# Group norm's mean moved from the recurrence's output to the value projection

## The chip, the cores and the metric

The kernel runs on one NeuronCore of a Trainium2 chip. TensorE (PE, with its weight loads PEld), VectorE (DVE), ScalarE (ACT) and GpSimd (POOL) each work through a queue of their own in a fixed order. SyncE (SP) issues nearly all DMAs, also in order. The metric is device time in microseconds (us) of one execution.

## The reference, cut to what matters

The model is a trunk of two layers on 1024 tokens of width 1024: an RWKV-7 time mixer, then differential attention, each followed by a gated per-layer embedding. The change lies in the first layer. Each of its 16 heads (64 wide) keeps a 64x64 state that a delta rule updates from token to token. The state's output `y` goes through a group norm of each head:

```
proj = einsum('bsgd,dgc->bsgc', xm, w_in)          # r, k, v, gate
def step(state, inp):
    sa    = einsum('bhij,bhj->bhi', state, kk_t)
    state = state * w_t - sa[..., None] * b_t + v_t[..., None] * k_t
    y_t   = einsum('bhij,bhj->bhi', state, r_t)
...
mean = jnp.mean(y, axis=-1, keepdims=True)          # over the 64 of a head
var  = jnp.mean(jnp.square(y - mean), axis=-1, keepdims=True)
y    = (y - mean) * rsqrt(var + GN_EPS) * ln_w + ln_b
bonus = sum(rh * kh * r_k, axis=-1, keepdims=True) * vh
y    = (y + bonus) * silu(gate) @ w_out
```

The index `i` of `state[i, j]` comes only from `v`, and every step is linear in it. So the mean of `y` over a head is what the same recurrence would give from the mean of `v` over that head. The bonus uses `v` as it is.

## The kernel before, in words

**Stages.** The span falls into these: norm and low-rank projections, then the projections of k and r, then **the v stage** (331 to 457 us), then the gate projection (to 572 us), then **the scan** over 16 chunks of 64 tokens with group norm and output projection woven in (to about 940 us), then the second half of the first layer, attention, and the tail.

**The v stage.** It runs over 4 column blocks `q` of 256 and 8 token blocks `i` of 128, 32 blocks in all. Each has 24 matmuls into a PSUM tile of tag `mm` (4 buffers), one ACT copy of 128x256 into an SBUF tile `vst` (L664) and one DMA from SP to the scratch tensor `v_d` (L665). `vst` takes a buffer of the tag `xmt`, of which there are 3; `make_xm`, which prepares the inputs of the next projection (L221), takes its buffers from the same 3. Woven between these blocks and the gate projection by `tick` are the triangular inverses that the scan needs: `inv_pb` (PE and DVE), `inv_diag` with a long chain of small DVE operations `tm`, `tb` (L558, L560) and two transposes (L570, L575), and `inv_merge` (PE products `pg` and `po`, L593, fed by ACT copies `prhs` and `pairs`). They come in four quarters.

**The scan.** For chunk c, `chain_x`, `chain_u` and `chain_s` are the recurrence; `stage1` prepares chunk c+1, with `mh` giving `pm` on PE (L185) and the masked `m` on DVE (L188). `vload` reads v of a chunk (L837). After every second chunk `d1_pieces` normalises 128 tokens: `norm` (a DVE reduction, a small scale and a subtraction, L953 to L955, then a square on ACT, L957), `norm2` (from L963), `turn` (PE transposes `ytr`, L981) and the output projection `op`. It also loads v (L944) for the bonus. ACT writes `y` from PSUM at L923. `d1_pieces` runs 8 times.

**Order.** The program is written in the order of these pieces, and a planner with its own estimates of cost settles the order on each engine. That order is fixed before the run, and an engine waits at an instruction until its inputs and its buffer are there.

Of the kernel before, what the change touches and what calls it, by code (L numbers as in the profile page):

```python
# [11 lines left out]
F32 = mybir.dt.float32  # L12
# [3 lines left out]
AF = mybir.ActivationFunctionType  # L16
ALU = mybir.AluOpType
AX = mybir.AxisListType
# [3 lines left out]
P = 128  # L22
D = 1024
SEQ = 1024
KT = D // P
NT = SEQ // P
L = 64
# [10 lines left out]
def trunk(ctx: ExitStack, tc: tile.TileContext, A, out):  # L38
    nc = tc.nc
    V, S, G, T = nc.vector, nc.scalar, nc.gpsimd, nc.tensor  # L40

    cp = ctx.enter_context(tc.tile_pool(name="const", bufs=1, reuse_waits="tile"))
    dp = ctx.enter_context(tc.tile_pool(name="scratch", bufs=1, space=DRAM))
# [8 lines left out]
    kb_d = dp.tile([KT, P, NCH, 2, L], F32, name="kb_d")  # L52
    kkr_d = dp.tile([KT, P, NCH, 2, L], F32, name="kkr_d")
    v_d = dp.tile([SEQ, D], F32, name="v_d")
    sg_d = dp.tile([KT, P, SEQ], F32, name="sg_d")

    def rsqrt(y, a, t):
# [9 lines left out]
    def mean_eps(ms, ss, n, eps):  # L67
        V.tensor_scalar(out=ms, in0=ss, scalar1=1.0 / n, scalar2=eps, op0=ALU.mult, op1=ALU.add)
# [5 lines left out]
    def mm3(ps, ah, al, bh, bl, start, stop):  # L74
        T.matmul(ps, lhsT=ah, rhs=bh, start=start, stop=False)  # L75
        T.matmul(ps, lhsT=ah, rhs=bl, start=False, stop=False)  # L76
        T.matmul(ps, lhsT=al, rhs=bh, start=False, stop=stop)  # L77
# [19 lines left out]
    ssn = cp.tile([P, NT, 16], F32, name="ssn")  # L97
# [95 lines left out]
    with NB("ab") as ab, NP("psab") as pp:  # L193
# [23 lines left out]
        def wpair(nm):  # L217
            return (ab.tile([P, D], F32R, tag="wh", name=nm + "h", bufs=3),
                    ab.tile([P, D], F32R, tag="wl", name=nm + "l", bufs=3))
# [14 lines left out]
        def make_half(g, hf):  # L234
            return [make_xm(g, kt, hf) for kt in range(KT)]

        def wload(nm, src):
            r = wraw(nm + "r")
            nc.sync.dma_start(out=r, in_=src)
            h, lo = wpair(nm)  # L240
            split(h, lo, r)
            return h, lo
# [21 lines left out]
        with NB("pl") as pl:  # L264
# [56 lines left out]
            for nm, cf in (("c", cA), ("p", cB)):  # L321
                t = wraw("lw" + nm).rearrange("p (k c) -> p k c", c=P)
                for g in range(2):
                    gs = slice(g * L, g * L + L)
                    V.tensor_tensor(out=t[:, :, gs], in0=wa[:, :, gs],
                                    in1=cf[:, 4 + g].unsqueeze(2).to_broadcast([P, KT, L]), op=ALU.mult)
                h, lo = wpair("lws" + nm)
# [308 lines left out]
        def tick(n):  # L636
            due[0] += n
            while due[0] >= 1.0:
                due[0] -= 1.0
                next(bg, None)  # L640
# [10 lines left out]
        for q in range(4):  # L651
            wv = [wload(f"wv{q}{k2}", A["wv"][q, k2].rearrange("p k c -> p (k c)")) for k2 in range(2)]
            for i in range(NT):
                x_ = xm[i // 4]
                ts_ = slice((i % 4) * P, (i % 4 + 1) * P)
                ps = pp.tile([P, 512], F32, tag="mm", name=f"v{q}{i}", bufs=4)[:, 0:256]
                for kt in range(KT):
                    if kt == 4 and (q or i > 3):
                        tick(TV)
                    cs = slice((kt % 4) * 256, (kt % 4) * 256 + 256)  # L660
                    mm3(ps, x_[kt][0][:, ts_], x_[kt][1][:, ts_], wv[kt // 4][0][:, cs], wv[kt // 4][1][:, cs],
                        kt == 0, kt == KT - 1)
                st = ab.tile([P, 512], F32, tag="xmt", name=f"vst{q}{i}", bufs=3)[:, 0:256]
                S.copy(st, ps)  # L664
                nc.sync.dma_start(out=v_d[i * P:(i + 1) * P, q * 256:(q + 1) * 256], in_=st)  # L665
                if q or i > 2:
                    tick(TV)
                if q == 3 and i % 4 == 3:
                    new[i // 4] = make_half(3, i // 4)
# [146 lines left out]
    with NB("d") as d, NP("psco") as pp:  # L816
# [17 lines left out]
        def vload(c):  # L834
            vu = co.tile([P, 2, 4, 2, L], F32, tag="vu", name=f"vu{c}", bufs=2)
            for st in range(2):
                nc.sync.dma_start(out=vu[64 - 64 * st:128 - 64 * st, st].rearrange("p j h l -> p (j h l)"),  # L837
                                  in_=v_d[c * L:(c + 1) * L, st * 512:st * 512 + 512])
            vus[c] = vu

        half_ = lambda x: slice(64 * x, 64 * x + 64)
# [1 line left out]
        def chain_x(c):  # L843
# [3 lines left out]
            if c + 1 < NCH:  # L847
                vload(c + 1)
# [87 lines left out]
        def d1_pieces(i):  # L936

            w = D1[i]
            rows = slice(i * P, (i + 1) * P)
            y = w["y"]  # L940

            def load():
                w["v"] = dt_("vn", f"vn{i}")
                nc.sync.dma_start(out=w["v"], in_=v_d[rows, :])  # L944
                w["sg"] = kview(dt_("sg", f"sg{i}"))
                nc.sync.dma_start(out=w["sg"], in_=sg_d[:, :, rows].rearrange("j p t -> p j t"))
                w["x"] = dt_("xr", f"xr{i}")
                nc.sync.dma_start(out=w["x"], in_=A["x"][rows, :])

            def norm():  # L950
                y3 = y.rearrange("p (h l) -> p h l", l=L)
                st = d.tile([P, 4, 16], F32, tag="gst", name=f"gst{i}", bufs=2)
                V.tensor_reduce(out=st[:, 0], in_=y3, axis=AX.X, op=ALU.add)  # L953
                V.tensor_scalar(out=st[:, 0], in0=st[:, 0], scalar1=-1.0 / L, scalar2=None, op0=ALU.mult)
                V.tensor_tensor(out=y3, in0=y3, in1=st[:, 0].unsqueeze(2).to_broadcast([P, 16, L]), op=ALU.add)  # L955
                sq = dt_("sq", f"ysq{i}")
                S.activation(sq, y, AF.Square)  # L957
                w["st"], w["sq"] = st, sq

            def norm2():  # L960
                st, sq, vn = w["st"], w["sq"], w["v"]
                y3 = y.rearrange("p (h l) -> p h l", l=L)
                V.tensor_reduce(out=st[:, 1], in_=sq.rearrange("p (h l) -> p h l", l=L), axis=AX.X, op=ALU.add)  # L963
                mean_eps(st[:, 1], st[:, 1], L, 64e-5)
                rsqrt(st[:, 2], st[:, 1], st[:, 3])
                V.tensor_tensor(out=y3, in0=y3, in1=st[:, 2].unsqueeze(2).to_broadcast([P, 16, L]), op=ALU.mult)
                G.tensor_tensor(out=y, in0=y, in1=lnw, op=ALU.mult)
                v3 = vn.rearrange("p (h l) -> p h l", l=L)
                G.tensor_tensor(out=v3, in0=v3, in1=bon[:, i].unsqueeze(2).to_broadcast([P, 16, L]), op=ALU.mult)
                V.tensor_tensor(out=y, in0=y, in1=vn, op=ALU.add)  # L970
                w["gh"] = kview(dt_("gh", f"gh{i}", 2, F32R))
                w["gl"] = kview(dt_("gl", f"gl{i}", 2, F32R))
                w["ps"] = [None, None]

            def turn(hf):
                yg, gh, gl = w["sg"], w["gh"], w["gl"]
                ps = pp.tile([P, 4, P], F32, tag="t", name=f"ytr{i}{hf}", bufs=2)
                hs = slice(hf * 4, hf * 4 + 4)
                for q in range(4):
                    kt = hf * 4 + q  # L980
                    T.transpose(ps[:, q], y[:, kt * P:(kt + 1) * P], ident)  # L981
                for q in range(4):
                    kt = hf * 4 + q
                    V.scalar_tensor_tensor(out=yg[:, kt], in0=ps[:, q], scalar=vec["ln_b"][:, kt:kt + 1],
                                           in1=yg[:, kt], op0=ALU.add, op1=ALU.mult)
                split(gh[:, hs], gl[:, hs], yg[:, hs], V)

            def mms(hf, k0):
                gh, gl = w["gh"], w["gl"]
                cs = slice(hf * 512, hf * 512 + 512)  # L990
                if k0 == 0:
                    w["ps"][hf] = pp.tile([P, 512], F32, tag="mm", name=f"op{i}{hf}", bufs=2)
                for kt in range(k0, k0 + 2):
                    mm3(w["ps"][hf], gh[:, kt], gl[:, kt], wo[kt][0][:, cs], wo[kt][1][:, cs],
                        kt == 0, kt == KT - 1)
                if k0 + 2 == KT:
                    V.tensor_tensor(out=w["x"][:, cs], in0=w["ps"][hf], in1=w["x"][:, cs], op=ALU.add)
                    if hf == 1:
                        nc.sync.dma_start(out=h1_d[rows, :], in_=w["x"])
                        sq = dt_("sq", f"h1sq{i}")  # L1000
                        S.activation(sq, w["x"], AF.Square, accum_out=ss1[:, i:i + 1])

            def mk(hf, k0):
                return lambda: mms(hf, k0)

            m0, m1 = [[(mk(hf, k0), 1280) for k0 in range(0, KT, 2)] for hf in range(2)]
            return ([(load, 100), (norm, 1000)], [(norm2, 1000)],
                    [(lambda: turn(0), 600), (lambda: turn(1), 600)] + m0, m1)

# [625 lines left out]
```

## Time and profile before

| | |
|---|---|
| median of 3 runs | 1829.12 us (1828.71 to 1832.35) |
| profiled execution, its time | 1828.3 us |
| its span in the profile | 1826.5 us |
| mean granted TensorE clock | 0.963 |
| PE busy | 1684.7 us (92%) |
| DVE busy | 1350.9 us (74%) |
| ACT busy | 760.4 us (42%) |
| POOL busy | 634.5 us (35%) |

The span runs from the first to the last instruction; what lies around it is 1.8 us here. Busy shares are means over stages with different limits. Full granted clock is 1.00 (2.4 GHz), and 0.50 is the lower of the two levels (1.2 GHz).

### The profile page before, as it was taken

The page shows a single profiled execution, that of the slowest core. Times are in us where ns is not written, and L with a number is a line of the kernel's source. Part 1 is how long each engine was busy: PE and PEld are TensorE (multiplying, and loading weights), DVE is VectorE, ACT ScalarE, POOL GpSimd, SP SyncE. Part 2 cuts the span into 40 slices and gives each one's busy share as a digit, 9 for nine tenths or more (in the row PEclk, how much of TensorE's full clock was granted, in tenths as well). Part 3 has the DMA queues.
Part 4 walks back from the last instruction along what each step waited for, and adds up shares of the span by engine and source line. Part 5 has one row for each costly group of instructions (what it writes and reads, how often), then busy time and mean ns, then how long its engine had stood idle before and what let it go on. Part 6 is the DMA issues. An engine that isn't in the chain of part 4 may idle for free.

```text
span 1826.5 us, 30473 instructions
## 1 busy us (share of the span) xinstructions
PE 1684.7 (92%) x11320; PEld 1397.6 (77%) x11320; DVE 1350.9 (74%) x3083; ACT 760.4 (42%) x1594; POOL 634.5 (35%) x705
## 2 busy tenths in 40 slices
PE   6899999898897988898899999899999999999998
PEld 5677778887676877777678878788888888777786
DVE  7878954698994687666766747887877878856665
ACT  6566543346344332223333434444444444544332
POOL 4436644224324355455310333323323323311200
PEclk9999999998998989999999999999999999999999
DMA  7125444434225534444243411101101101431121
GB/s 267 41 61 166 129 106 109 125 102 119 73 67 186 186 127 127 122 129 131 97 172 128 132 51 39 54 7 56 56 7 56 53 10 56 154 99 34 58 93 69
DMA packets 164401, 175.97 MB, mean 96 GB/s; under 512 B 74845, under 2 KB 127837, under 8 KB 164254
## 3 DMA queue, kind: packets, MB, share of 16 engines
q1 hardware_dynamic: 161950, 169.84, 30.2%
q10 hardware_dynamic: 2304, 4.20, 0.6%
q8 instruction: 89, 1.46, 0.4%
q14 instruction: 58, 0.48, 0.1%
HBM read 124.19 MB, written 49.81 MB: 95 GB/s over the span
## 4 chain that ended last, share of the span: by engine, by line
PE 51%; DVE 10%; ACT 2%; issue 1%; DMA 0%; POOL 0%; ACTq 0%; DVEq 0%
PE qkv L75 6%; PE qkv L76 6%; PE qkv L77 6%; PE av L1359 3%; PE sc L1319 2%; PE sc L1320 2%; PE fg L75 2%; PE fg L76 2%; PE fg L77 2%; PE op L75 2%; PE op L77 2%; PE op L76 2%; PE do L75 1%; PE pg L76 1%; PE pg L77 1%; PE do L76 1%
## 5 line engine op out<-in xcount | busy, mean ns | idle before, releaser
L1329 ACT ACTIVATE e<-sc,mx 128x256 f32<-128x256 f32 (+7 forms) x128 | 94.0, 738 | 111.0 <-DVE mx L1326 60.0
L1273 POOL TENSOR_TENSOR rp<-rp,rq 128x128 f32<-128x128 f32 x64 | 34.8, 543 | 237.6 <-DVE rq L1268 189.7
L1359 PE MATMUL av<-vh,aT 128*128 128x128 f32 x576 | 81.1, 280 | 6.3 <-DVE aT L1355 6.3
L1359 PEld LDWEIGHTS av<-vh,aT 128*128 128x128 f32 x576 | 75.6, 195 | 12.8 <-DVE aT L1355 8.9
L1325 DVE TENSOR_REDUCE mxs<-sc 128x1 f32<-128x128 f32 (+6 forms) x112 | 74.2, 682 | 0.5
L1319 PE MATMUL sc<-k,q 128*128 128x512 f32 (+2 forms) x192 | 71.5, 379 | 2.2 <-ACT e L1329 2.2
L229 DVE SCALAR_TENSOR_TENSOR xmt<-hT,cB,xmt 128x512 f32<-128x512 f32 x64 | 63.5, 1012 | 6.6 <-ACT xmt L228 6.3
L1320 PE MATMUL sc<-k,q 128*128 128x512 f32 (+2 forms) x192 | 64.8, 348 | 0.0
L1361 ACT ACTIVATE o<-av,r 128x128 f32<-128x128 f32 x64 | 23.5, 367 | 88.4 <-PE av L1359 88.4
L875 POOL TENSOR_TENSOR spl<-state,plast 64x256 f32<-64x256 f32 x60 | 41.4, 690 | 49.6 <-DVE state L910 42.7
L1341 DVE SCALAR_TENSOR_TENSOR e<-e,r,e 128x128 f32<-128x128 f32 (+3 forms) x64 | 56.5, 883 | 1.2
L560 DVE TENSOR_TENSOR tb<-tb,tm 128x31 f32<-128x31 f32 (+15 forms) x124 | 53.9, 435 | 3.6
L558 DVE TENSOR_TENSOR tm<-tb,nb 128x31 f32<-128x31 f32 (+15 forms) x124 | 53.9, 434 | 3.6
L188 DVE TENSOR_TENSOR m<-pm,mmask 128x512 f32<-128x512 f32 x64 | 41.1, 682 | 20.0 <-PE pm L185 19.7
L1301 POOL CAST q<-q 64x128 fp32r<-64x128 f32 x128 | 38.5, 302 | 49.4 <-PE sc L1320 45.6
L1267 DVE TENSOR_TENSOR rp<-qkv,rc 128x256 f32<-128x256 f32 x64 | 27.1, 423 | 38.3 <-PE qkv L77 30.1
L1292 POOL CAST k<-k 64x256 fp32r<-64x256 f32 x64 | 26.1, 408 | 83.7 <-ACT k L1290 82.5
L185 PE MATMUL pm<-kkr,kb 64*128 64x128 f32 x512 | 50.8, 307 | 3.1 <-ACT kbn L176 2.2
L1355 DVE COPY aT<-at 128x512 f32<-128x512 f32 (+2 forms) x96 | 52.0, 550 | 1.1 <-PE at L1353 0.4
L185 PEld LDWEIGHTS pm<-kkr,kb 64*128 64x128 f32 x512 | 40.4, 203 | 12.9 <-issue 6.0
L1353 PE MATMUL at<-ident,e 128*128 128x128 f32 x288 | 47.4, 277 | 2.8 <-DVE e L1341 2.3
L923 ACT COPY y<-xy 64x512 f32<-64x512 f32 x32 | 18.6, 580 | 71.4 <-PE xy L916 71.0
(1180 smaller groups left out, 6001.5 us busy)
## 6 DMA issues: line engine op xcount, KB each, us to landing
pp_d<-ppo SPq DMA_DIRECT2D x32, 256.0 KB, 2.3
kb_d<-kb SPq DMA_DIRECT2D x16, 512.0 KB, 2.6
kkr<-kkr_d SPq DMA_DIRECT2D x32, 256.0 KB, 3.2
kb<-kb_d SPq DMA_DIRECT2D x32, 256.0 KB, 3.3
x<-in_x SPq DMA_DIRECT2D x8, 512.0 KB, 5.5
kkr_d<-ep SPq DMA_DIRECT2D x16, 256.0 KB, 2.6
kkr_d<-rt SPq DMA_DIRECT2D x16, 256.0 KB, 2.6
bb<-kb_d SPq DMA_DIRECT2D x32, 128.0 KB, 2.6
```

The source lines that it names most:

```text
L75: T.matmul(ps, lhsT=ah, rhs=bh, start=start, stop=False)
L76: T.matmul(ps, lhsT=ah, rhs=bl, start=False, stop=False)
L77: T.matmul(ps, lhsT=al, rhs=bh, start=False, stop=stop)
L185: ms.append(T.matmul(pm[h][:, p_], lhsT=kb[hs, p_], rhs=kkr[hs, p_], start=True, stop=True))
L229: V.scalar_tensor_tensor(out=t, in0=hT[:, kt, half(hf)], scalar=cB[:, g, kt:kt + 1], in1=t, op0=ALU.mult, op1=ALU.add)
L558: V.tensor_tensor(out=tv, in0=tb[:, j:j + 1, 0:w].to_broadcast([P, n, w]), in1=nb[:, j + 1:32, j:j + 1].to_broadcast([P, n, w]), op=ALU.mult)
L1319: T.matmul(ps[:, b0:b1], lhsT=q1[:, m, ts_], rhs=k1[:, m, b0:b1], start=True, stop=False)
L1320: T.matmul(ps[:, b0:b1], lhsT=q0[i % 2][:, m], rhs=k2[:, b0:b1], start=False, stop=True)
L1325: V.tensor_reduce(out=seed, in_=ps[:, 0:n - P], axis=AX.X, op=ALU.min)
L1329: S.activation(e[:, 0:n], ps[:, 0:n], AF.Exp, scale=-1.0, bias=mx, accum_out=l_[:, m:m + 1])
L1341: V.scalar_tensor_tensor(out=es[0][:, 0:n], in0=es[1][:, 0:n], scalar=r[:, 1:2], in1=es[0][:, 0:n], op0=ALU.mult, op1=ALU.add)
L1359: T.matmul(po, lhsT=aT[kb // 4][:, kb % 4], rhs=c["vh"][:, kb], start=(kb == 0), stop=(kb == i))
```

## The change

In the v stage ACT now evacuates each block in four pieces of 64 columns, one for each head, and sums each piece as it goes. POOL scales the four sums by -1/64 and adds them to the piece, which gives centred v beside plain v. Both go to HBM, v to `v_d` and centred v to a new scratch tensor `vc_d`. The recurrence reads `vc_d`; the bonus still reads `v_d`. In `norm` the three DVE operations fall away, and ACT squares `y` as it is.

The sums stand in `ssn`, a tile whose earlier contents have been used up by then.

```diff
+    vc_d = dp.tile([SEQ, D], F32, name="vc_d")
...
-                st = ab.tile([P, 512], F32, tag="xmt", name=f"vst{q}{i}", bufs=3)[:, 0:256]
-                S.copy(st, ps)
-                nc.sync.dma_start(out=v_d[i * P:(i + 1) * P, q * 256:(q + 1) * 256], in_=st)
+                vt = ab.tile([P, 2, 4, L], F32, tag="xmt", name=f"vst{q}{i}", bufs=3)
+                sm = ssn[:, i, 4 * q:4 * q + 4]
+                for h in range(4):
+                    S.activation(vt[:, 0, h], ps[:, h * L:(h + 1) * L], AF.Copy, accum_out=sm[:, h:h + 1])
+                G.tensor_scalar(out=sm, in0=sm, scalar1=-1.0 / L, scalar2=None, op0=ALU.mult)
+                G.tensor_tensor(out=vt[:, 1], in0=vt[:, 0], in1=sm.unsqueeze(2).to_broadcast([P, 4, L]), op=ALU.add)
+                for x, dst in enumerate((v_d, vc_d)):
+                    nc.sync.dma_start(out=dst[i * P:(i + 1) * P, q * 256:(q + 1) * 256],
+                                      in_=vt[:, x].rearrange("p h l -> p (h l)"))
...
             for st in range(2):
                 nc.sync.dma_start(out=vu[64 - 64 * st:128 - 64 * st, st].rearrange("p j h l -> p (j h l)"),
-                                  in_=v_d[c * L:(c + 1) * L, st * 512:st * 512 + 512])
+                                  in_=vc_d[c * L:(c + 1) * L, st * 512:st * 512 + 512])
...
             def norm():
-                y3 = y.rearrange("p (h l) -> p h l", l=L)
                 st = d.tile([P, 4, 16], F32, tag="gst", name=f"gst{i}", bufs=2)
-                V.tensor_reduce(out=st[:, 0], in_=y3, axis=AX.X, op=ALU.add)
-                V.tensor_scalar(out=st[:, 0], in0=st[:, 0], scalar1=-1.0 / L, scalar2=None, op0=ALU.mult)
-                V.tensor_tensor(out=y3, in0=y3, in1=st[:, 0].unsqueeze(2).to_broadcast([P, 16, L]), op=ALU.add)
                 sq = dt_("sq", f"ysq{i}")
                 S.activation(sq, y, AF.Square)
```

## Rows read from the trace of the kernel before

**Rows 1.** Busy time by stage: us, then PE, PEld, DVE, ACT, POOL, PEclk, DMA, GB/s

```profile
331.00:457.00 126.00, 116.32 (x1339) 110.08 (x1340) 100.92 (x180) 59.30 (x105) 35.15 (x23) 0.91 0.45 120
457.00:572.00 115.00, 104.45 (x714) 81.22 (x713) 95.24 (x175) 49.87 (x78) 31.37 (x22) 0.94 0.29 91
628.00:945.00 317.00, 275.70 (x3078) 230.59 (x3077) 229.13 (x453) 94.69 (x144) 153.96 (x150) 0.94 0.43 134
```

**Rows 2.** Waits of PE in the scan, 572 to 945 us: total, times, longest

```profile
PE ytr L981 <- DVE m L188: 16.8, 6, 4.1
...
PE prt L162 <- DVE m L188: 3.0, 4, 0.9
```

**Rows 3.** Timeline around one group norm: start, us, engine, line [idle before <-releaser]

```profile
705.55 1.22 DVE L953 TENSOR_REDUCE gst<-y 128x16 f32<-128x1024 f32 x1
...
706.52 0.72 POOL L157 TENSOR_TENSOR pr<-kkr,kb 128x256 f32<-128x256 f32 x1
706.80 0.48 DVE L954 TENSOR_SCALAR gst<-gst 128x16 f32<-128x16 f32 x1
707.31 1.23 DVE L955 TENSOR_TENSOR y<-y,gst 128x1024 f32<-128x1024 f32 x1
...
709.72 1.22 DVE L963 TENSOR_REDUCE gst<-ysq 128x16 f32<-128x1024 f32 x1 [1.18 <-ACT ysq L957]
710.97 1.29 DVE L188 TENSOR_TENSOR m<-pm,mmask 128x512 f32<-128x512 f32 x2
...
711.72 0.82 PE L981 MATMUL ytr<-ident,y 128*128 128x128 f32 x4 [4.04 <-DVE m L188]
```

**Rows 4.** The same columns as rows 1, after a long and a short wait

```profile
712.00:716.00 4.00, 4.00 (x44) 3.51 (x43) 2.78 (x13) 1.79 (x3) 0.73 (x1) 0.57 0.00 0
...
816.00:820.00 4.00, 3.73 (x71) 3.03 (x72) 1.41 (x3) 1.75 (x5) 3.27 (x4) 1.00 1.01 280
```

**Rows 5.** ACT by line and shape: busy us, mean ns | idle before

```profile
L1269 ACT COPY vh<-qkv 128x128 f32<-128x128 f32 x64 | 16.8, 263 | 56.0 <-DVE rq L1268 50.1 <-DVE ost L63 3.0 <-DVE ost L65 2.7
L1364 ACT ACTIVATION_READ_ACCUMULATOR os<-o 128x1 f32 x64 | 12.2, 191 | 0.0
L664 ACT COPY vst<-v 128x256 f32<-128x256 f32 x32 | 11.6, 372 | 44.6 <-PE v L77 28.4 <-issue 13.8 <-ACT pairs L567 0.9
```

**Rows 6.** POOL's nearest operations: by source line (ns min/median/max), and by line

```profile
L158 POOL TENSOR_TENSOR pr<-pr,vecs x32: 602/614/1686, 556.6 to 890.5; 128x256 f32<-128x256 f32 x32
...
L204 POOL TENSOR_SCALAR hka<-vecs 128x8 f32<-128x8 f32 x1 | 0.2, 234 | 0.0
```

**Rows 7.** Timeline of DVE and POOL in the v stage

```profile
408.10 0.42 DVE L560 TENSOR_TENSOR tb<-tb,tm 128x255 f32<-128x255 f32 x1
408.31 2.48 POOL L72 TENSOR_TENSOR wv31l<-wv31r,wv31h 128x1024 fp32r<-128x1024 f32 x1 [15.82 <-PE v L77]
408.56 2.51 DVE L558 TENSOR_TENSOR tm<-tb,nb 128x256 f32<-128x256 f32 x1
```

**Rows 8.** Timeline of PE at its waits in the v stage

```profile
331.43 0.58 PE L75 MATMUL v<-wv00h,xm_1h 128*128 128x256 f32 x1 [4.87 <-ACT vst L664]
...
389.40 2.15 PE L593 MATMUL pg<-prhs,pairs 64*64 64x32 f32 x64 [3.12 <-ACT prhs L574]
...
430.24 2.05 PE L593 MATMUL pg<-prhs,pairs 64*64 64x32 f32 x64 [1.28 <-ACT prhs L574]
```

**Rows 9.** Timeline of ACT: first and last of twenty evacuations, and the last ones

```profile
356.10 0.37 ACT L664 COPY vst<-v 128x256 f32<-128x256 f32 x1 [5.24 <-issue]
...
420.36 0.37 ACT L664 COPY vst<-v 128x256 f32<-128x256 f32 x1 [3.27 <-PE v L77]
...
454.31 0.93 ACT L664 COPY vst<-v 128x256 f32<-128x256 f32 x3
458.94 0.73 ACT L228 ACTIVATE xmt<-hT,cA 128x512 f32<-128x512 f32 x1 [3.70 <-DMA v_d<-vst]
```

**Rows 10.** Where the inverse's last transpose stands, by source line

```profile
L575 DVE STREAM_TRANSPOSE ti<-tb x4: 1867/1968/2005, 386.7 to 548.9; 128x1024 f32<-128x1024 f32 x4
```

## The prediction

> **What bounds the kernel now.** I read the busy time by stage first, because the change takes work from one stage and puts it into another. In the scan PE is busy 275.70 of 317 us, in the v stage 116.32 of 126, in the gate projection 104.45 of 115 [rows 1]. PE sets the pace in all three, and what matters is why it sometimes stands still. The list of PE's waits in the scan names one cause above the others: the transposes `ytr` wait 16.8 us in 6 places for DVE's masking `m` [rows 2]. The timeline shows what DVE does in such a place. PE stands still from 707.68, 4.04 us before 711.72. DVE first works through the three operations of the mean (705.55 to 708.54), waits 1.18 us for ACT's square, reduces it, and only then does `m` [rows 3]. So the mean stands on the path here, though DVE is busy only 229.13 of 317 us in this stage [rows 1].
>
> The v stage is bound by two things in turn. PE waits 3.12 and 1.28 us at two `pg` products for `prhs`, which ACT copies from DVE's inverse [rows 8]; there DVE sets the pace. From 457 to 572 DVE is busy 95.24 of 115 us [rows 1], and the inverse's last transpose starts at 548.9 [rows 10]: whatever delays DVE's inverse delays the scan. ACT and POOL, busy 59.30 and 35.15 of 126 us [rows 1], have room on average.
>
> **What the scan loses.** Eight groups lose 1.22, 0.48 and 1.23 us on DVE [rows 3], some 23 us in all, and the square may start as soon as `y` is there. PE's gap cannot shrink to nothing: `m` itself follows `pm`. The waits of the other chunks, where no norm stands between, are 3.0 us in 4 places, the longest 0.9 [rows 2]; I take 0.87 for what stays. The gain is 16.8 - 6 x 0.87 = 11.6 us. The clock comes on top: after a long gap it is 0.57 for 4 us, which costs 0.43 x 4 = 1.7 us, and after a short one it is 1.00 [rows 4]. Four of the six gaps are followed by such a dip, 6.8 us together; I take 5, since a dip that other waits cause would stay. The scan's gain is 16.6 us. From below it is bounded by nothing (DVE could put `norm2` in the same place), from above by the 23 us of DVE work and the 6.8 us of clock, 30 us.
>
> **What the v stage gets.** ACT's copy of 0.372 us becomes four sums of 128x64. No such row exists. Between 128x128 (0.263) and 128x256 (0.372) the step is 0.109 for 128 columns, so 64 columns should take 0.21, and at most 0.263. Each ends with a read of the accumulator, 0.191 [rows 5]. Four are 1.60 us, at most 1.82: 1.23 to 1.45 us more for a block, 39 to 46 us more in the stage. Behind them on ACT's queue are the copies for the inverse and `make_xm`.
>
> POOL gets a scale of 128x4 (nearest row 0.234) and an addition of 128x256 with a broadcast (0.614) [rows 6], 0.85 us a block, 27 us in all. Mostly it idles there, so its own time is hidden. SP gets 32 more issues, and 4.2 MB more are written (32 x 128 KB) while the DMA engines are busy 0.45 of the time [rows 1]; I count that at nothing, and it is hidden as long as inputs are loaded a block ahead. The buffer of `xmt` is held longer: by the additional 1.23 on ACT, 0.85 on POOL and one more issue, some 2.4 us.
>
> Three of these reach the path.
>
> First, PE waits at 331.43 until ACT has emptied the first block [rows 8]. Emptying takes 1.23 us longer: +1.2 (0 to 1.5).
>
> Second, DVE's inverse. While POOL runs a 2.48 us subtraction, a DVE operation that takes 0.42 next to it takes 2.51 [rows 7], so DVE loses 2.09, or 84% of POOL's time. A short one shows the same: DVE's 0.48 us scale ends with POOL's 0.72 us product [rows 3]. Of the 32 blocks, 20 are emptied between 356.10 and 420.36 [rows 9], 19 of them while DVE runs `tm` and `tb`, and the last 3 fall into its next quarter: 22. Taking 84% of 0.614, 0.5 us each, and nothing for the scale, which is so short that it mostly fits while DVE finishes its own operation, this is 11 us. It goes through to the end, because PE already waits at both `pg` and DVE has little slack after 457. If DVE's time were lost where DVE waits anyway, it is 0; if POOL's whole 0.85 counts, 19.
>
> The Trainium skill has a stricter rule here (SBUF — State Buffer, section Who interferes with whom): a DVE instruction with two SBUF inputs contends with a GpSimd instruction that reads SBUF, and whichever comes first holds the shared pair of ports for its whole length. By it, both POOL operations of a block cost DVE their whole time, 22 x 0.85 = 18.7 instead of 11. The long operation in rows 7 lies between: 84%.
>
> Third, the end of the stage. ACT empties three blocks from 454.31, and its next preparation waits 3.70 us at 458.94 for the DMA that frees a buffer [rows 9]. With buffers held 2.4 us longer, that comes about 2.5 us later, and the first gate matmuls with it: +2.5 (0 to 8).
>
> Sum: 1.2 + 11 + 2.5 = 14.7 us. The profiled execution took 1828.3 us, so 1828.3 - 16.6 + 14.7 = 1826.4 us. The median of the runs shown is 0.8 us above it; on that scale I expect 1827.0 us, 2.1 less than before.
>
> **Rivals.**
>
> The queue on ACT (slower). Between the evacuations at 420.36 and 454.31 [rows 9] ACT works mostly on copies for the inverse and on `make_xm`. If the planner puts four or more of the longer evacuations among them, each adds 1.23 us to a chain for which PE and DVE wait, 5 to 10 us, and the four blocks waiting at the start of the stage add up to 3.7 more. That is 9 to 14 on top of my sum: 1836 to 1841 us. For it: buffers come free later, and `make_xm` waits for one already [rows 9]. Against it: PSUM has four buffers, and ACT has half its time free [rows 1]. It decides from four blocks on. Chance 0.17.
>
> The whole lock (no better than before). If both POOL operations block DVE for all of their time, the second term is 18.7: 1827.0 + 7.7 = 1834.7 us, with 1831 to 1837 for 18 to 24 blocks. Against it is the 84%; for it, that two operations per block have to win the ports twice. The rule of the Trainium skill above would make this the forecast. Chance 0.12.
>
> The lock is hidden (clearly faster). If POOL's additions fall where DVE transposes or waits, or PE gets other work at the `pg`, only 3.7 us of the loss stay: 1827.0 - 11 = 1816 us (1811 to 1820). For it: ACT's order decides when the additions come, and near each `pg` they bunch. Against it: 19 of 20 fall on `tm` and `tb`. Chance 0.18.
>
> The scan's gap stays (slower). If another DVE operation, say the reduction of the squares, takes the place in front of `m`, PE waits on as before, and only some 3 us of the gain are left: 1827.0 + 13.6 = 1841 us (1836 to 1843). Against it: the square needs only `y`, 3 us earlier than now [rows 3]. Chance 0.08.
>
> **How the numbers follow.** The forecast, with both terms near the sizes above, has chance 0.45; its own range is 1820 to 1834 us, since each term may be off by some 5. About 0.2% of the time, 3.7 us, is what a measurement of this kernel can tell from no change: 1825.5 to 1832.8 us. Of the forecast's 0.45 I put 0.20 below, 0.20 within and 0.05 above. The hidden lock is all faster (0.18). Of the whole lock 0.05 is within and 0.07 slower; the ACT queue (0.17) and the remaining gap (0.08) are slower. Faster 0.38, same 0.25, slower 0.37. The range from 1812 to 1842 us takes in the main part of all these and leaves out the best of the hidden lock and the worst of the ACT queue.
>
> **What would show it.** Right, if in the new profile PE's waits for `m` at `ytr` fall from 16.8 to about 5 us and the clock after them is near 1.00; if ACT's pieces take 0.21 and 0.19 us; if DVE's `tm` and `tb` show some 20 stretched operations of about 1 us in the v stage, PE's waits at `pg` grow by 5 us each, and the inverse's last transpose comes some 14 us later. Wrong, if the transpose stays within 4 us of 548.9, or moves by over 20, or if `ytr` still waits 3 us or more at a time.

## The result, and the profile after

The changed kernel takes 1845.38 us (median of 4 runs, 1841.97 to 1849.25), the kernel before beside it 1830.47 (4 runs): 1.0082 of it, interval 1.0068 to 1.0097. It is slower by 14.9 us, above the forecast range. The profiled execution is the longest of the four, 1849.25 us with a span of 1847.5, so the parts below add up to 21.0 us of span and not to 14.9.

I cut both spans at the same instructions: the first matmul of the v stage, the last transpose `ea` of the inverse, the first and the last `xy` with `vu` and `m` in `chain_x` (L864 in before; the scan), and the first `qkv`. The last chunk's outputs and the last norm come behind the last of these `xy`, so the scan and the stage behind it are also worth reading as one stretch: 449.0 us before, 462.0 after. These starts are from the profiles, in us.

| stretch | before | after | difference |
|---|---|---|---|
| start to first `v` | 314.4 | 316.6 | +2.2 |
| first `v` to last `ea` | 232.4 | 241.0 | +8.6 |
| last `ea` to first `xy` | 44.9 | 45.0 | +0.1 |
| first to last `xy`, the scan | 309.5 | 316.7 | +7.2 |
| last `xy` to first `qkv`, the stage behind the scan | 139.5 | 145.3 | +5.8 |
| first `qkv` to the end | 785.8 | 782.9 | -2.9 |

Nothing is changed in the first and the last stretch: 2 to 3 us are the difference of two executions. The loss is in three places, and in the one where 16.6 us were to be gained, the scan, 7.2 were lost.

Busy time by stage of the changed kernel, as in [rows 1]:

```profile
331.00:457.00 126.00, 109.99 (x1310) 105.41 (x1312) 98.86 (x171) 68.44 (x288) 56.25 (x77) 0.90 0.49 135
457.00:572.00 115.00, 102.30 (x646) 79.12 (x639) 103.71 (x180) 55.18 (x114) 39.06 (x33) 0.92 0.29 89
628.00:945.00 317.00, 273.82 (x3138) 229.73 (x3137) 206.08 (x426) 91.28 (x140) 141.25 (x153) 0.91 0.42 131
```

DVE has indeed lost 23 us in the scan (229.13 to 206.08), and POOL has gained its 21 in the v stage. PE has gained nothing in the scan: its clock fell from 0.94 to 0.91. PE's waits from 572 to 945 us say why; the first and the third row answer to the two of [rows 2]:

```profile
PE ytr L987 <- DVE m L189: 18.0, 6, 3.6
PE xy L864 <- ACT y L932: 7.1, 1, 7.1
PE prt L163 <- DVE m L189: 6.8, 7, 1.8
```

PE waits for `m` as before, 18.0 us at `ytr` where it was 16.8, and 6.8 at `prt` where it was 3.0. The one wait of 7.1 was 5.2 in before. None of the transposes uses `m`: in the scan `pm`, `kbt`, `prt` and `ytr` share the two PSUM buffers of tag `t`, and it is `m` that reads `pm` and so gives its buffer back. Whether one more buffer for this tag would end the waits was not tried. The timeline at one of the six places, which answers to [rows 3] (start, us, engine, line, idle before and releaser):

```profile
713.50 1.06 ACT L963 ACTIVATE ysq<-y 128x1024 f32<-128x1024 f32 x1
...
714.59 1.22 DVE L969 TENSOR_REDUCE gst<-ysq 128x16 f32<-128x1024 f32 x1 [0.70 <-ACT ysq L963]
714.90 1.48 PE L186 MATMUL pm<-kkr,kb 64*128 64x128 f32 x16
...
715.71 0.61 POOL L159 TENSOR_TENSOR pr<-pr,vecs 128x256 f32<-128x256 f32 x1
715.85 0.50 DVE L69 TENSOR_SCALAR gst<-gst 128x16 f32<-128x16 f32 x1
716.28 1.05 POOL L172 TENSOR_TENSOR kbp<-kb,plast 128x512 f32<-128x512 f32 x1
716.38 0.97 DVE L59 TENSOR_SCALAR gst<-gst 128x16 int32<-128x16 int32 x1
...
718.64 0.18 DVE L66 SCALAR_TENSOR_TENSOR gst<-gst 128x16 f32<-128x16 f32 x1
718.85 0.69 DVE L189 TENSOR_TENSOR m<-pm,mmask 128x512 f32<-128x512 f32 x1
...
719.54 0.68 DVE L189 TENSOR_TENSOR m<-pm,mmask 128x512 f32<-128x512 f32 x1
719.59 1.12 PE L987 MATMUL ytr<-ident,y 128*128 128x128 f32 x4 [3.21 <-DVE m L189]
```

The mean's three operations are gone, and `pm`, of which `m` is made, is there at 716.38. But from 715.85 to 718.82 DVE now works off the next part of the norm, nine small operations on `gst` (L69 to L66: the mean square's scaling and the Newton steps of its inverse root), two of them lengthened beside POOL's products (0.50 and 0.97 us, where the others take 0.17 or 0.18), and only then `m`. In [rows 3] these nine stood behind `m`. The same lies behind five of the six waits. The four microseconds after this wait are at the lower clock, as in [rows 4]:

```profile
720.00:724.00 4.00, 4.00 (x43) 3.55 (x42) 3.46 (x10) 1.79 (x3) 0.63 (x1) 0.50 0.00 0
```

After five of the six waits the clock is at 0.50 for four microseconds; in before it is at 0.57 to 0.59 after four of them. From the first to the last `xy`, before and after:

```profile
591.70:901.20 309.50, 274.86 (x3285) 231.88 (x3284) 214.19 (x422) 86.83 (x138) 152.31 (x159) 0.94 0.42 131
602.60:919.30 316.70, 279.25 (x3283) 234.75 (x3284) 199.43 (x403) 87.41 (x139) 142.39 (x159) 0.92 0.42 127
```

So of the 7.2 us, PE stands still for 2.8 more (37.45 for 34.64), and is busy for 4.4 more with the same matmuls, at a lower mean clock.

The v stage, by line (busy us, mean ns, idle before), answers to [rows 5, 6]; the two DVE rows are those of the inverse, from 331 to 575 us:

```profile
L669 ACT ACTIVATE vst<-v 128x64 f32<-128x64 f32 x128 | 26.7, 226 | 33.5 <-issue 11.2 <-POOL vst L671 8.4 <-DMA vc_d<-vst 5.0
L669 ACT ACTIVATION_READ_ACCUMULATOR vst<-v 128x1 f32 x128 | 25.8, 211 | 0.0
L671 POOL TENSOR_TENSOR vst<-vst,ssn 128x256 f32<-128x256 f32 x32 | 21.4, 670 | 2.4
L670 POOL TENSOR_SCALAR ssn<-ssn 128x4 f32<-128x4 f32 x32 | 8.7, 271 | 36.2 <-ACT vst L669 31.6 <-DMA bb<-kb_d 3.3
```

```profile
L559 DVE TENSOR_TENSOR tm<-tb,nb 128x31 f32<-128x31 f32 (+15 forms) x124 | 58.7, 473 | 3.6
L561 DVE TENSOR_TENSOR tb<-tb,tm 128x31 f32<-128x31 f32 (+15 forms) x124 | 57.0, 460 | 3.6
```

The same view of before has 53.9 us for each of the two, so the inverse's small operations have become 115.7 - 107.8 = 7.9 us longer. PE's waits for the inverse have grown less at `pg` (6.7 us for 4.9, 331 to 575 us) than at the products before it, `pb`, which wait for DVE's `nq` (11.1 for 5.6). The first block's evacuation and its effect on PE (starts on ACT, then PE's wait, which answers to the first row of [rows 8]):

```profile
333.22 0.20 ACT L669 ACTIVATE vst<-v 128x64 f32<-128x64 f32 x1
333.33 0.19 ACT L669 ACTIVATION_READ_ACCUMULATOR vst<-v 128x1 f32 x1
333.42 0.21 ACT L669 ACTIVATE vst<-v 128x64 f32<-128x64 f32 x1
...
333.92 0.22 ACT L669 ACTIVATION_READ_ACCUMULATOR vst<-v 128x1 f32 x1
```

```profile
334.19 0.58 PE L76 MATMUL v<-wv00h,xm_1h 128*128 128x256 f32 x1 [5.41 <-ACT vst L669]
```

Each piece takes the 0.2 us that I estimated, but the next starts 0.10 us after it: the eight operations are done in 0.92 us, not 1.60.

### The profile page after: what moved, and what is told of

Its sections match the earlier page's. It is cut to its first block, busy times and chain, and to the rows that moved or that the text cites. A ratio compares the mean times of both kernels' runs of the same rounds, so it can differ in the third digit from the quotient of the medians.

```text
span 1847.5 us, 30849 instructions
## 1 busy us (share of the span) xinstructions
PE 1692.4 (92%) x11320; PEld 1404.0 (76%) x11320; DVE 1337.9 (72%) x3059; ACT 777.9 (42%) x1818; POOL 649.8 (35%) x769
## 4 chain that ended last, share of the span: by engine, by line
PE 53%; DVE 10%; ACT 2%; DMA 1%; issue 1%; POOL 0%; SPq 0%; POOLq 0%; ACTq 0%; DVEq 0%
PE qkv L76 6%; PE qkv L78 6%; PE qkv L77 6%; PE av L1365 3%; PE sc L1325 2%; PE sc L1326 2%; PE fg L76 2%; PE fg L78 2%; PE fg L77 2%; PE op L76 2%; PE pg L78 1%; PE do L76 1%; PE op L77 1%; PE pg L76 1%; PE pg L77 1%; PE op L78 1%
## 5 line engine op out<-in xcount | busy, mean ns | idle before, releaser
L559 DVE TENSOR_TENSOR tm<-tb,nb 128x31 f32<-128x31 f32 (+15 forms) x124 | 58.7, 473 | 3.6
L158 POOL TENSOR_TENSOR pr<-kkr,kb 128x256 f32<-128x256 f32 x32 | 23.5, 733 | 81.6 <-issue 68.8
L78 PE MATMUL pg<-pwg,pl 128*128 128x512 f32 x112 | 45.4, 407 | 4.0 <-DVE pl L769 4.0
```

Of the source, the lines that this page charges most:

```text
L559: V.tensor_tensor(out=tv, in0=tb[:, j:j + 1, 0:w].to_broadcast([P, n, w]), in1=nb[:, j + 1:32, j:j + 1].to_broadcast([P, n, w]), op=ALU.mult)
```

## The experiments

Theory 1: the gain in the scan is lost to the planner's order. With the mean gone, the rest of the norm moves up in DVE's queue to the place in front of `m`. Theory 2: the scan gains as forecast, and the v stage alone loses it. The twelve runs, with the ratio to the kernel before on the same chip (95% interval; the ratio is not in every row the quotient of the medians), and stretches of one profiled execution in us:

| run | median us | ratio | first `v` to first `xy` | scan | behind the scan | `ytr` waits for `m` |
|---|---|---|---|---|---|---|
| before | 1830.1 to 1830.5 | 1 | 277.3 | 309.5 | 139.5 | 16.8 |
| after | 1845.38 | 1.0082 (1.0068 to 1.0097) | 286.0 | 316.7 | 145.3 | 18.0 |
| e1 | 1838.68 | 1.0040 (1.0028 to 1.0052) | 277.0 | 316.1 | 144.8 | 18.1 |
| e2 | 1847.01 | 1.0097 (1.0083 to 1.0112) | 288.3 | 318.7 | 139.5 | 20.3 |
| e3 | 1834.13 | 1.0025 (1.0016 to 1.0033) | 286.7 | 297.2 | 148.1 | 3.7 |
| e4 | 1826.34 | 0.9976 (0.9967 to 0.9985) | 278.0 | 299.6 | 148.4 | 3.7 |
| f1 | 1830.55 | 1.0000 (0.9991 to 1.0009) | 282.0 | 299.6 | 147.8 | 3.7 |
| f2 | 1834.07 | 1.0023 (1.0014 to 1.0032) | 284.6 | 298.9 | 147.7 | 3.7 |
| e5 | 1837.82 | 1.0049 (1.0034 to 1.0064) | 277.9 | 313.7 | 140.2 | 9.8 |
| e6 | 1839.75 | 1.0050 (1.0037 to 1.0063) | 284.1 | 298.8 | 146.2 | 3.7 |
| e7 | 1828.96 | 0.9997 (0.9986 to 1.0007) | 291.9 | 297.2 | 143.0 | 3.7 |
| e8 | 1838.34 | 1.0049 (1.0036 to 1.0062) | 283.9 | 300.2 | 149.1 | 3.7 |
| e9 | 1830.25 | 1.0002 (0.9991 to 1.0012) | 286.5 | 297.4 | 141.4 | 3.7 |
| e10 | 1826.12 | 0.9969 (0.9957 to 0.9981) | 277.4 | 304.8 | 141.1 | 4.7 |

The profiled execution of e7 is the longest of its twelve runs, 4.7 us over their median, and its first stretch is 5.2 us longer than e3's, whose code there is the same. In this stretch DVE, ACT and POOL work in the same order in after, e2, e3, e6 and e7, and it takes 284.1 to 291.9 us; before, e1, e4, e5 and e10, again alike, take 277.0 to 278.0. A difference of a few us between two profiles of that stretch therefore says little by itself.

**One half of the change alone (e1, e2).** e1 takes the three operations out of before and changes nothing else; e2 has the change without that removal.

```diff
 # e1: before
-                V.tensor_reduce(out=st[:, 0], in_=y3, axis=AX.X, op=ALU.add)
-                V.tensor_scalar(out=st[:, 0], in0=st[:, 0], scalar1=-1.0 / L, scalar2=None, op0=ALU.mult)
-                V.tensor_tensor(out=y3, in0=y3, in1=st[:, 0].unsqueeze(2).to_broadcast([P, 16, L]), op=ALU.add)
```

> The kernel before, in which only the three mean operations of the norm are left out (the reduction, its scaling and the subtraction), so the mean is not subtracted anywhere; the v stage is that of before. Theory 1 (in the scan the place that the three operations leave on VectorE is taken by the second norm's chain of small operations, which now stands in front of the masking m): no gain in the scan, the time 1826 to 1838, the six PE waits of ytr on m at 17 to 20 us together, as in the changed kernel (18.0) and before (16.8). Theory 2 (the scan gains what was forecast and the v stage alone loses it): about 1814, 16 us less than before, and the waits of ytr on m at 5 us.

> The changed kernel's v stage (four activations with sums, the scaling and addition on GpSimd, two stores, the recurrence on centred v), with the three mean operations of the norm put back. Theory 1: the loss of the stages of v and of the gates alone, 8 to 11 us by the first ea (6.5 us later in the changed kernel) and the last ea (10.8 later), of which 2.2 arose ahead of the change: 1836 to 1842, and the scan as before. Theory 2: the whole loss and more, 1846 to 1862, with the scan as before.

Taking three operations away and adding nothing made the kernel 8.6 us slower by the medians. The scan grew by 6.6 us, with the waits for `m` at 18.1: theory 1, and the mechanism stands without any change to v. The stage behind the scan grew by 5.3, which neither theory had. e2 does not fit theory 1's number: 1847 where 1836 to 1842 were expected. Its first stretch is 11.0 us longer, as expected, but its scan is 9.2 longer too, with the same operations in it as before. The time lies in theory 2's range, but theory 2 too had the scan as before. Its waits for `m` are 4.09, 4.09, 1.64, 4.04, 2.38 and 4.09 us, before's 1.62, 4.04, 4.09, 1.88, 1.13 and 4.08. In before the planner put `m` ahead of the reduction of the squares in two of six places, those with 1.62 and 1.88; in e2 in none whole and in one by half (1.64). So an edit two stages earlier moved `m` too.

**The order restored (e3, e4).** e3 is the changed kernel, e4 is e1, each with one edge: the norm's chain may start only after the last `m` of the chunk beside it. The edge orders two instructions of one queue and makes neither wait for data.

```diff
 # e3, e4
-                mean_eps(st[:, 1], st[:, 1], L, 64e-5)
+                e = V.tensor_scalar(out=st[:, 1], in0=st[:, 1], scalar1=1.0 / L, scalar2=64e-5, op0=ALU.mult, op1=ALU.add)
+                if 2 * i + 2 in mi:
+                    turns([mi[2 * i + 2], e])
```

> The changed kernel with one edge of order: the second norm's chain (from the scaling of the mean square on) stands behind the last masking m of the chunk beside it, where before it stood. Theory 1: the waits of ytr on m fall from 18.0 to 5 to 8 us, and the time to 1832 to 1838, 8 to 13 us under the changed kernel, still at or above before by what the v stage costs. Theory 2: no change against the changed kernel, 1843 to 1848, since the scan is not where the time is lost.

> The kernel before without the three mean operations (the mean is not subtracted) and with the same edge of order: the chain behind m. Theory 1: this is what the removal could give to the scan with the order kept: the waits of ytr on m at 5 to 8 us, the time 1814 to 1822, 8 to 16 us under before. Theory 2: the same time as the same kernel without the edge, within 3 us. A third reading, that the scan is bound by PE's clock and by work of its own whoever comes first on VectorE: both at 1826 to 1832.

The edge is worth 11.3 us in the changed kernel and 12.3 in e1. PE's waits of e3 in the scan, and the clock in the four microseconds after the wait that answers to the one shown:

```profile
PE ytr L990 <- DVE m L190: 3.7, 6, 0.8
```

```profile
715.00:719.00 4.00, 3.54 (x46) 2.74 (x46) 3.92 (x14) 1.74 (x3) 1.59 (x3) 1.00 0.45 133
```

The waits are 0.6 us each and the clock after them is full; over the scan it is 0.98 where after has 0.92. The scan is 12.3 us shorter than before in e3, 9.9 in e4: most of the 16.6 that I had forecast exists, once the order is set. But e4 is only 3.7 us faster in all, short of the 1814 to 1822 expected, since the stage behind the scan is 8.9 us longer.

**The v stage taken apart (f1, f2).** Both start from e3.

```diff
 # f1
-                G.tensor_scalar(out=sm, in0=sm, scalar1=-1.0 / L, scalar2=None, op0=ALU.mult)
-                G.tensor_tensor(out=vt[:, 1], in0=vt[:, 0], in1=sm.unsqueeze(2).to_broadcast([P, 4, L]), op=ALU.add)
...
-                                      in_=vt[:, x].rearrange("p h l -> p (h l)"))
+                                      in_=vt[:, 0].rearrange("p h l -> p (h l)"))
 # f2
-                for h in range(4):
-                    S.activation(vt[:, 0, h], ps[:, h * L:(h + 1) * L], AF.Copy, accum_out=sm[:, h:h + 1])
-                G.tensor_scalar(out=sm, in0=sm, scalar1=-1.0 / L, scalar2=None, op0=ALU.mult)
+                S.copy(vt[:, 0], ps.rearrange("p (h l) -> p h l", l=L))
+                G.tensor_scalar(out=sm, in0=vt[:, 0, :, 0], scalar1=-1.0 / L, scalar2=None, op0=ALU.mult)
```

> The changed kernel with the chain behind m (median 1834.1 us), without the two GpSimd operations of the v stage: ACT's four sums and both stores stay, the second store writes the same uncentred v, so the mean is not subtracted. With neither sums nor GpSimd work the same scan took 1826.3, so the v stage costs 7.8 us there. If GpSimd's additions cost it by holding up VectorE's tm and tb: 1827 to 1829, tm and tb back at 434 ns mean, the last ea some 8 us earlier. If ACT's longer evacuation and the longer held buffers cost it: 1832 to 1834, and only tm and tb change.

> The same kernel with one copy of 128x256 on ACT in place of the four sums; GpSimd's scaling and addition stay in place and in size (they take the first column of each head for its sum, so the mean is not subtracted). If GpSimd holding up VectorE is the cost: 1832 to 1834, tm and tb still at 460 to 473 ns. If ACT's sums are: 1827 to 1829. If both add up: near 1830 in both kernels.

By ratio to before, e4 with neither is at 0.9976, the sums without POOL's work (f1) at 1.0000, POOL's work without the sums (f2) at 1.0023, both (e3) at 1.0025. Of 0.0049, some 9 us, f2 brings 8.6 and f1 4.4, and these do not add up. Both of them keep the second store, which e4 does not have. If that store, or the longer held buffer, cost some 4 us, POOL's work would cost 4.6 and the sums 0.4, and all would add up; no run has the second store alone, so this is open. The first stretch has the same order, 278.0, 282.0, 284.6 and 286.7, but with a spread of 284.1 to 291.9 for the code of e3 the last step says nothing. f1's 1830.55 us lies between the two times expected. How POOL costs it, from the timeline of the changed kernel in the v stage:

```profile
372.44 0.42 DVE L561 TENSOR_TENSOR tb<-tb,tm 128x255 f32<-128x255 f32 x1
372.89 0.72 DVE L559 TENSOR_TENSOR tm<-tb,nb 128x256 f32<-128x256 f32 x1
373.65 0.42 DVE L561 TENSOR_TENSOR tb<-tb,tm 128x256 f32<-128x256 f32 x1
```

```profile
372.02 0.46 POOL L670 TENSOR_SCALAR ssn<-ssn 128x4 f32<-128x4 f32 x1 [1.81 <-ACT vst L669]
372.56 0.77 POOL L671 TENSOR_TENSOR vst<-vst,ssn 128x256 f32<-128x256 f32 x1
```

A `tm` that takes 0.42 us takes 0.72 beside POOL's addition. It ends 0.28 us after the addition (373.61 and 373.33), and so does the `tm` of [rows 7] after POOL's long subtraction (411.07 and 410.79). What is lost is in both the rest of POOL's operation when `tm` starts, less 0.14 us: 0.44 gives 0.30, 2.23 gives 2.09. The `tb` that was already under way when the addition started lost nothing. This holds throughout: 22 of the 32 additions run beside `tm` and `tb`, each holds up one of them, and against the median of the same shape in before the loss is the rest less 0.14 or 0.15 us every time, 6.8 us in all or 0.31 each. The scales, where nothing else of POOL ran beside them, cost nothing. The other 1.1 of the 7.9 us come from POOL's other operations, which hold up 15 of the small ones where it was 13.

Without POOL's work (f1) the two are back at 54.8 and 53.5 us, with it (f2) at 53.3 and 58.5. That is 4.0 us more than before, though the 22 additions of f2 cost 7.1: POOL's other operations happen to hold up `tm` and `tb` for 3.1 less there.

**The amount or the place (e5, e10).** Both are the kernel before, with the mean's operations in the norm and one edge. In e5 the reduction of the squares stands behind the last `m`, in e10 the reduction of the mean stands behind all four.

```diff
 # e5
-                V.tensor_reduce(out=st[:, 1], in_=sq.rearrange("p (h l) -> p h l", l=L), axis=AX.X, op=ALU.add)
+                e = V.tensor_reduce(out=st[:, 1], in_=sq.rearrange("p (h l) -> p h l", l=L), axis=AX.X, op=ALU.add)
+                if 2 * i + 2 in mi:
+                    turns([mi[2 * i + 2], e])
 # e10
-                V.tensor_reduce(out=st[:, 0], in_=y3, axis=AX.X, op=ALU.add)
+                e = V.tensor_reduce(out=st[:, 0], in_=y3, axis=AX.X, op=ALU.add)
+                for x in mi.get(2 * i + 2, ()):
+                    turns([x, e])
```

> The kernel before, nothing removed, with one edge of order: the reduction of the squares (norm2) stands behind the last masking m of the chunk beside it. If what PE waits for at ytr is the place of m in VectorE's order and not the amount of VectorE's work: the waits of ytr on m fall from 16.8 to 4 to 8 us and the time to 1820 to 1827. If the three mean operations themselves, which stay ahead of m, set the gap: no change, 1828 to 1832. If the place is won and the stage behind the scan gives it back, as in the kernels whose mean was removed: scan 8 to 10 us shorter, time 1826 to 1829.

> The kernel before, nothing removed, with all four maskings m of a chunk ahead of the mean's reduction of the norm beside it, on VectorE. In the run where only the reduction of the squares stood behind m, the three mean operations still stood ahead of it and PE's waits for m were 9.8 us at ytr and 6.5 at xy. If place decides and not amount: the waits of ytr on m at 3 to 5 us, the scan 298 to 305 us (before 309.5), the time 1820 to 1828. If the 23 us of the mean operations cost the scan wherever they stand: the scan 308 to 314 us, the time 1829 to 1838.

e5 failed. The planner kept the mean's operations ahead of `m` and moved the half of `m` that was free to move behind the reduction: 9.8 us at `ytr`, and 6.5 at `xy`, where before has no such row among its longest. e10 is what e5 was meant to be. Its DVE around the place of [rows 3], and PE:

```profile
714.27 1.29 DVE L189 TENSOR_TENSOR m<-pm,mmask 128x512 f32<-128x512 f32 x2 [2.23 <-PE pm L186]
...
715.02 0.65 PE L984 MATMUL ytr<-ident,y 128*128 128x128 f32 x4 [0.78 <-DVE m L189]
715.48 1.21 DVE L954 TENSOR_REDUCE gst<-y 128x16 f32<-128x1024 f32 x1
...
718.71 1.21 DVE L958 TENSOR_TENSOR y<-y,gst 128x1024 f32<-128x1024 f32 x1
```

DVE waits 2.23 us for `pm` with the norm's work at hand, and PE waits 0.78 us for `m` in place of 4.04. With all of the mean's work still there, e10 is 4.4 us faster than before by the medians and the fastest here that leaves nothing out. e4, which has not even the mean, is at 0.9976 to its 0.9969, and the intervals overlap. That does not make the removal worthless once the order is set: e4's scan is 5.2 us shorter (304.8 to 299.6), and the 7.3 that it gives back behind the scan are in good part the fault that the next runs take up. From the first `xy` to the first `qkv` before takes 449.0 us, e4 448.0, e10 445.9, and e7, without the mean's operations and with both places set, 440.2. No run joins e4 with the edges of e7.

**Behind the scan (e6, e7).** All kernels with the mean in the norm take 139.5 to 141.1 us there, those without it and without an edge there 144.8 to 149.1. PE and ACT of e3 say why:

```profile
922.90 1.09 PE L766 MATMUL ptr<-ident,n 128*128 128x128 f32 x8 [0.23 <-DVE n L1128]
927.16 0.80 PE L76 MATMUL pg<-pwg,ph 128*128 128x512 f32 x1 [3.16 <-ACT ph L769]
...
932.30 0.80 PE L78 MATMUL pg<-pwg,pl 128*128 128x512 f32 x1 [3.06 <-DVE pl L770]
```

```profile
925.34 1.15 ACT L731 ACTIVATE pwg<-pwg06r,vecs 128x1024 fp32r<-128x1024 f32 x1 [2.87 <-DMA pwg06r<-in_pwg]
926.51 0.60 ACT L769 ACTIVATE ph<-ptr 128x512 fp32r<-128x512 f32 x1
```

`ph`, the input of the gate's first product, could be made when `ptr` ends at 923.99. It stands behind a weight row that ACT awaits from its DMA until 925.34. In before ACT had `ph` at 926.03, ahead of that row at 928.27, and PE waited 0.25 us for it. In after it stands behind the row as in e3, and PE waits 2.08 us for `ph` and 4.05 for `pl`.

```diff
 # e6, e7: a and b are the two operations on row pwg06, gi["ph"] the pairs ph, pl of the first block
+            if nm == "pwg06":
+                for x, y in gi["ph"]:
+                    turns([x, a])
+                    turns([y, b])
 # e6 alone
-                    nc.sync.dma_start(out=dw0[k4], in_=A["dqkvg"][0, k4])
+                    turns([gi["pwg07"][0], nc.sync.dma_start(out=dw0[k4], in_=A["dqkvg"][0, k4])])
 # e7 alone
+            if nm == "pwg07":
+                for x, y in gi["ph"]:
+                    turns([x, a])
```

> The changed kernel with the chain behind m (1834.1), and with the order of the stage behind the scan fixed too: ACT's and VectorE's work on the gate row pwg06 stands behind the first ph and pl, and the loads of dw0 behind those of the gate rows. From the end of the scan to the first qkv the kernels without the mean operations take 145 to 148 us where before takes 139.5. If the order on ACT and VectorE (ph and pl queued behind a weight row that waits for its transfer) makes this: the waits of pg on ph and pl (3.2 and 3.1) fall under 1 us each, the stretch to 142 to 144, the time to 1828 to 1831. If PE waits there only because the scan ends earlier than the weights can be there: no change, 1833 to 1836.

> The changed kernel with the chain behind m (1834.1), and behind the scan ACT's first ph and VectorE's first pl ahead of the work on both late gate rows, pwg06 and pwg07; the loads keep their order. In the run with the edge on pwg06 alone ph stood behind pwg07's row instead and PE waited 6.8 us. If ph and pl queued behind a row that waits for its transfer are what the stage behind the scan loses: PE's waits of pg on ph and pl at 1 us or less each, from the scan's last xy to the first qkv 141 to 144 us in place of 148, the time 1827 to 1831. If it is lost whoever comes first, since the rows themselves are late: 146 to 149 us and 1833 to 1836.

e6 failed in the way of e5: with pwg06 held back, the planner put pwg07 in front of `ph`, and PE waited 6.8 us instead of 3.2 and 3.1.

```profile
928.39 1.15 ACT L730 ACTIVATE pwg07r<-pwg07r,vecs 128x1024 f32<-128x1024 f32 x1 [6.24 <-DMA pwg07r<-in_pwg]
929.56 0.60 ACT L775 ACTIVATE ph<-ptr 128x512 fp32r<-128x512 f32 x1
```

With both rows held back (e7) the wait for `ph` is 0.25 us, one for `pl` stays at 2.81, and the median falls by 5.2 us against e3:

```profile
929.25 0.51 PE L76 MATMUL pg<-pwg,ph 128*128 128x512 f32 x1 [0.25 <-ACT ph L778]
933.26 0.79 PE L78 MATMUL pg<-pwg,pl 128*128 128x512 f32 x1 [2.81 <-DVE pl L779]
```

So 5.1 of the 8.6 us that e3 loses behind the scan are the same fault in another place; the other 3.5 stay open, the wait for `pl` among them. After the first `qkv` e6 takes another 3.6 us more than e3 (788.7 to 785.1); its held-back loads of `dw0` feed that stretch, but I did not try them by themselves.

**Centring without POOL (e8, e9).** e8 is e3 with the scale and four additions of a bias on ACT, e9 is e7 with the same.

```diff
 # e8, e9
-                G.tensor_scalar(out=sm, in0=sm, scalar1=-1.0 / L, scalar2=None, op0=ALU.mult)
-                G.tensor_tensor(out=vt[:, 1], in0=vt[:, 0], in1=sm.unsqueeze(2).to_broadcast([P, 4, L]), op=ALU.add)
+                S.activation(sm, sm, AF.Copy, scale=-1.0 / L)
+                for h in range(4):
+                    S.activation(vt[:, 1, h], vt[:, 0, h], AF.Identity, bias=sm[:, h:h + 1])
```

> The changed kernel with the chain behind m (1834.1), v centred on ACT instead of GpSimd: the scaling of the four sums and four additions of a bias (128x64 each) run on ACT, nothing on GpSimd; v and centred v are both stored. If GpSimd holding up VectorE is most of the v stage's cost (the last ea 10 us late with it, 3 us without): tm and tb at 430 to 445 ns, the last ea 4 to 7 us later than before, 1829 to 1832. If ACT's time counts as well: five more operations of about 0.2 us a block make ACT's queue the bound, the last ea 10 us later or more, 1835 to 1842.

> Both edits at once: the changed kernel with the chain behind m, v centred on ACT, and ph and pl ahead of the late gate rows. If both gains hold and add: 1823 to 1828, a changed kernel that beats the kernel before. If one of them is nothing: 1829 to 1833. If both are: 1834 to 1838.

DVE is no longer held up (`tm` and `tb` 109.0 us together, 107.8 in before), and the last `ea` came 3.8 us later than before and not 9.9 as in e3. But from there to the first `xy` it is 49.1 us in place of 44.9, and e8 is slower than e3. On ACT a block is dear: one that starts at 360.22 is done at 362.49, 2.27 us where the sums alone take 0.92. The addition of the bias takes 342 ns, and four together take 1.07 us. That this is what makes e8 slower is not shown: in the profiles its first `v` to first `xy` is 2.8 us shorter than e3's, and its scan 3.0 longer.

```profile
L673 ACT ACTIVATE vst<-vst,ssn 128x64 f32<-128x64 f32 x128 | 33.6, 342 | 0.5
```

e9 is at 1.0002, e7 at 0.9997: with the tail's order set, centring on ACT and on POOL cannot be told apart, and only one of e9's two gains came. The best form of the change that I found is even with the kernel before, and behind e10.

## Why the prediction was wrong

**The gain in the scan** is the step that failed. I took the mean's operations off the path and let `m` move up to `pm`: 11.6 us of waits and 5 of clock. Nothing of it came, and 7.2 us were lost, 2.8 of them with PE standing still and 4.4 with PE at work at a lower clock, where I had counted 5 us of clock as won. [Rows 3] held the answer: there `m` stands behind the reduction of the squares, which waits 1.18 us for ACT. My own sign of a wrong forecast, waits of 3 us or more at `ytr`, came in five of the six places. What kept PE waiting was a place in DVE's queue, given before the run, and not an amount of work ahead of it. e1 shows it without v. e3 and e4 show most of the forecast gain when the place is given back (12.3 and 9.9 us of scan), and e10 gets 4.7 with the mean's work untouched.

**The rival "the scan's gap stays"** is what happened, and I gave it 0.08. I named the reduction of the squares; it was the chain behind the reduction. Its argument against, that the square needs only `y` and comes 3 us earlier, may speak for it: the earlier the norm's inputs are there, the earlier the planner puts its work. That is my reading of the planner, and no run shows it. I also left 3 us of the gain to it; in the run the scan became longer. That the chain's first two operations are lengthened beside POOL's products, and so `m` behind them, is in the timeline (about 1.1 of the 3.21 us at the place shown, an estimate from the rows); I did not test it by itself.

**The v stage** was right in kind and too large: 8.7 us to the first `xy`, not 14.7 (6.8 to 14.6 over the five kernels with this stage). POOL's additions meet `tm` and `tb` 22 times, as I had it, but cost 0.31 us each and not 0.50: 6.8 us for 11. The 84% was no share: what DVE loses is the rest of POOL's operation, less 0.14 us, and of a short one a smaller part is left when DVE's next operation starts. Nor did PE's two waits at `pg` grow by 5 us each. The first evacuation costs 0.54 more (5.41 for 4.87) and not 1.2, since ACT's pieces overlap. The third term, 2.5 for buffers held longer, did not reach the first `xy`: from the last `ea` to it the time is the same. f1 and f2 bear POOL out as the larger part, with the second store open, which I had counted at nothing.

By the Trainium skill (SBUF — State Buffer, section Who interferes with whom) the port pair that VectorE and GpSimd share is an exclusive lock. The trace agrees: every `tm` or `tb` that an addition held up ended after it, 0.10 to 0.28 us behind. The page's words "for the whole instruction" stand at VectorE's two-port modes. The 18.7 us that I drew from the rule were too many, since DVE lost only the rest of each addition, and nothing to the scales.

**The stage behind the scan** had no term at all. It lost 5.8 us. There too an edit of the norm reordered the queues: `ph` stands behind the weight row in after as in e3, and in e3 the edges of e7 give 5.1 of 8.6 us back.

One slip in the working: 0.8 us above 1826.4 is 1827.2 and not 1827.0; nothing hangs on it. In sum, 8.7 in place of 14.7, +7.2 in place of -16.6, and 5.8 in place of nothing: 21.7 us, and with +2.2 and -2.9 in the two unchanged stretches the 21.0 by which the profiled span grew.

## What to carry to other kernels

Where a planner fixes the order of each queue, an edit changes two things, the work and the order, and the second can outweigh the first even where work is only taken away. Before a gain is booked for an operation removed from the front of a wait, ask which instruction the planner will put there; then set the order by an edge and measure the removal alone. The edge has to hold back everything that could take the place: e5 and e6 held back one candidate, and the next one stepped in.

## What I had not expected of the hardware

ACT overlaps short operations that follow each other: a copy of 128x64 with its sum takes 0.20 us and the read of the sum 0.19, but eight of them in a row start 0.10 us apart. With a bias from a tile the same shape took 342 ns where the copy with a sum took 223 (e8), and the four took longer together (1.07 us) than the eight (0.92). The first reads SBUF and the second PSUM, so which difference makes it is not shown.

And `tm` and `tb`, DVE operations with two inputs in SBUF, were held until POOL was done where they started beside one of its additions (22 times) or its long subtraction of [rows 7]. At the places shown they ended 0.28 us later, whether POOL's operation took 0.77 us or 2.48. So the cost was what was left of POOL's operation, and not a fixed share of it.
